# The values of four attention heads projected at once, with 512 columns, in a one-core decoder layer

## The chip, the cores and the metric

The kernel runs on one core of a Trainium2 chip. The metric is the device time of one execution in microseconds (us). Before the change three executions took 487.59, 487.79 and 489.74 us (median 487.79). In the text PE is the matrix engine, DVE the vector engine, ACT the scalar engine, POOL the GpSimd engine, SP the queue that issues nearly all DMA transfers.

## The reference, cut to what matters

One layer of a decoder on 512 rows of 1024 numbers, in float32. The normalized input is multiplied by one wide matrix `w_in`, whose columns are queries, keys, values and gates of two kinds of attention and two gates for the merge:

```python
h = rms_norm(x, norm_g[i])
proj = h @ w_in[i]
dq, dk, dv, dg, mq, mk, mv, mg, gates = split_in_proj(proj)   # 512 columns each, gates 2048
o_a = diff_attention(dq, dk, dv, lam, lam_init, subln_g[i]) * jax.nn.silu(dg)
y_a = o_a @ w_branch_diff[i]
o_b = moba_attention(mq, mk, mv) * jax.nn.silu(mg)
y_b = o_b @ w_branch_moba[i]
g_a, g_b = jnp.split(gates, N_BRANCHES, axis=-1)
merged = jax.nn.sigmoid(g_a) * y_a + jax.nn.sigmoid(g_b) * y_b
x = x + merged @ w_out[i]
x = x + jax.nn.sigmoid(x @ w_ple_gate[i]) * (p[i] @ w_ple[i])
return rms_norm(x, final_g)
```

The differential attention has 4 heads, each with two softmax maps over 64 dimensions and values of 128 columns (so 512 columns of values in all). The other kind (MoBA) has 8 heads of 64 dimensions; with 512 rows its selection reduces to causal attention, and the kernel treats two of its heads together.

## The kernel before, in words

**Three products for one.** Every float32 operand is split into a high part, rounded by a copy on ACT (`split`, `split_later`, line 102), and a low part, the rest, by a subtraction (line 104) on DVE or POOL. A product is then three matmuls (`mm3`, lines 115 to 117): high by high, high by low, low by high.

**Stages.** First the per-layer embedding product and the norm of `x`, four tiles of 128 rows; each normalized tile `h` is transposed on PE (line 362), and split into `hThi` and `hTlo`. Then eight pairs `j` = 0 to 7 (four differential heads, then four pairs of MoBA heads): for each, three tiles k, q and gate are projected (`project`, `proj_T`, 24 matmuls of 512 columns each), and k and q are rotated on DVE (`qk_tile`, lines 460 to 463, a rope of four instructions), split and copied between halves of the partitions on ACT and DVE (lines 468 to 483). After that come the merge gates, the branch products, the output product and the gated embedding.

**Values before.** `proj_v` makes the values of two differential heads or two pairs of MoBA heads with 256 columns: the transposed input is stationary, the weights move, 24 matmuls for each of four tiles of rows. The values of heads 0 and 1 are made whole ahead of pair 0, while the input tiles are still being normalized (`v_hook` transposes the next tile in the midst of it). Of the three others one half (two tiles of rows, 48 matmuls) stands ahead of each of the pairs 1 to 6. Ahead of pair 7 stands the first gate tile, `("a", 0)`.

**What sets the order.** The program is written out by a small clock: each group of matmuls of a projection calls `step()`, which ticks the clock and lets waiting generators go on: splits of weights, ropes, and `attention`. A tick is three matmuls of 512 columns, or six of 256. The attention of pair `j` starts two ticks after `project(j)`, and is laid between the projections of what follows, by `PLAN` (line 35): S0 to S3 are the score products of the four row tiles (lines 507, 509), E0 to E3 their maximum on DVE (line 517) and exponential on ACT (line 522), N0 to N3 the normalization on DVE (lines 527, 559, 560), T0 to T3 the transposes of the result on PE (line 533), and a number is a wait of so many ticks. After T3 and 5 ticks follow the product with the values (line 592), and the norm of the head (lines 596 to 609). Each engine executes its own instructions in the order in which they were written. So the number of ticks between two pairs decides where on DVE and ACT the work of one pair falls between that of the other: 32 for pairs 1 to 7 before the change (8 of values or gate tile and 24 of k, q and gate).

**Weights.** `units` lists the weight tiles of 512 KB in the order of use. `pump_loads` keeps up to six of them loaded by SP, `pump_split` splits them into five pairs of buffers, three tagged w and two tagged v; a unit is split when its tag has a free buffer. Up to the start of pair 0 the low part is made on DVE, then on POOL.

**PSUM.** Banks are shared by name: three `pj` for projections, two `sc` for scores, two `tp` for transposes, one `av`.

Of the kernel before, what the change touches and what calls it, by code (L numbers as in the profile page):

```python
# [12 lines left out]
AF = mybir.ActivationFunctionType  # L13
ALU = mybir.AluOpType

P = 128
S = 512
D = 1024
NT = S // P
# [22 lines left out]
def hybrid_block(ctx, tc, x, p, norm_g, w_in, lq1, lk1, lq2, lk2, subln_g, w_bd, w_bm,  # L42
# [15 lines left out]
    def bank(tag):  # L58
        return ps.tile([P, 512], F32, tag=tag, name=tag, bufs=BANKS[tag])
# [5 lines left out]
    def spawn(gen, after=0):  # L65
        running.append([clock[0] + after, gen])
# [47 lines left out]
    def mm3(acc, ahi, alo, bhi, blo, start, stop):  # L114
        T.matmul(acc, ahi, bhi, start=start, stop=False)  # L115
        T.matmul(acc, ahi, blo, start=False, stop=False)  # L116
        T.matmul(acc, alo, bhi, start=False, stop=stop)  # L117
# [4 lines left out]
    def add(key, tag, pieces, kn, cn):  # L122

        index[key] = len(units)
        units.append((tag, pieces, kn, cn))

    def add_cols(key, tag, c0):
        add(key, tag, [(0, KT, w_in[:, c0:c0 + P])], KT, P)

    def add_v(kind, jj):  # L130
        c0 = (C_DV, C_MV)[kind] + jj * 256
        for u in range(2):
            add(("v", kind, jj, u), "v", [(0, 4, w_in[u * 512:(u + 1) * 512, c0:c0 + 256])], 4, 256)

    def add_qkg(j, tags="www"):
        for n in (1, 0, 2):
            c0 = ((C_DQ, C_DK, C_DG), (C_MQ, C_MK, C_MG))[j // 4][n] + (j % 4) * P
            add(("qkg"[n], j), tags[n], [(0, KT, w_in[:, c0:c0 + P])], KT, P)
# [2 lines left out]
        while True:  # L141
            yield from "wwwvv"

    add_v(0, 0)
    add_qkg(0)
    for j in range(1, 7):
        if j % 2:
            add_v(*divmod((j + 1) // 2, 2))
        add_qkg(j)
    tags = tag_cycle()  # L150
    add_cols(("a", 0), next(tags), C_GA)
    add_qkg(7, [next(tags) for _ in range(3)])
    order = [(n, m) for m in range(3) for n in "ab"][1:] + [("o", m) for m in range(3)]
    order += [(n, m) for m in range(3, 8) for n in "abo"]
# [14 lines left out]
    def pump_loads(most=RAW):  # L169
        while state["loaded"] < min(len(units), state["split"] + RAW) and most:  # L170
            tag, pieces, kn, cn = units[state["loaded"]]
            r = wraw.tile([P, 1024], F32, name="raw").rearrange("p (k n) -> p k n", n=cn)
            for k0, k, src in pieces:
                Y.dma_start(r[:, k0:k0 + k], src.rearrange("(k p) n -> p k n", p=P))
            raw[state["loaded"]] = r
            state["loaded"] += 1
            most -= 1
# [35 lines left out]
    def step():  # L213

        since[0] += 1
        if since[0] >= PUMP and pump_split():
            since[0] = 0
        tick()

    def use(key):  # L220
        u = index[key]
        while ready.get(u) != 2:
            if state["split"] <= u:
                pump_split()
            tick()
        return parts[u]

    def free(key):
        free_bufs[units[index[key]][0]] += 1
# [8 lines left out]
    def proj_T(acc, key):  # L238
        w = use(key)
        for k in range(KT):  # L240
            mm3(acc, w[0][:, k], w[1][:, k], hThi[:, k], hTlo[:, k], k == 0, k == KT - 1)
            step()
        free(key)

    def proj_v(v, kind, jj, ts_, hook=None):

        heads = 4 if kind else 2
        keys = [("v", kind, jj, u) for u in range(2)]
        ws = [use(key) for key in keys]
        vt = v.rearrange("p (t h n e) -> p t h n e", t=NT, h=heads, n=2)  # L250
        for t in ts_:
            acc = bank("pj")[:, :256]
            ts = slice(t * P, (t + 1) * P)
            for k in range(KT):
                mm3(acc, hThi[:, k, ts], hTlo[:, k, ts], ws[k // 4][0][:, k % 4], ws[k // 4][1][:, k % 4],
                    k == 0, k == KT - 1)
                if k % 2:
                    step()
                if hook and k == KT // 2:
                    hook(t, False)  # L260
            spawn(split_later(vt[:, t, :, 0], vt[:, t, :, 1], acc.rearrange("p (h e) -> p h e", h=heads)))
            if hook:
                hook(t, True)
        if NT - 1 in ts_:
            for key in keys:
                free(key)

    def v_tile():
        return vbig.tile([P, 2048], F32R, name="v")

# [5 lines left out]
    with tc.tile_pool(name="norm", bufs=2) as npool:  # L276
# [17 lines left out]
        load_x(0)  # L294
        load_x(1)
        Y.dma_start(gb, norm_g[0:1].broadcast_to([P, D]))
        pump_loads(1)
        load_x(2)
        pump_loads(1)
        load_x(3)  # L300
        pump_loads()
        Y.dma_start(ropet, rope.rearrange("c p s -> p c s"))
# [133 lines left out]

        hook = {}
        since[0] = -4
        v = v_tile()
        proj_v(v, 0, 0, range(NT), v_hook)  # L440

        V.tensor_scalar(gsub, gsub, 0.5 * (1.0 - LAM_INIT), None, op0=ALU.mult)
        lsc = npool.tile([P, HD], F32, name="lsc", bufs=1)
# [103 lines left out]
    def attention(kind, j, qkg, v):  # L547

        q, k, g = qkg
        sm = [Softmax(q, k, i) for i in range(NT)]  # L550
        pts = [pt_tiles() for _ in range(1 + kind)]

        def norm(i):
            e, rc = sm[i].e, sm[i].recip()
            if kind:
                for s in range(2):
                    V.tensor_scalar(e[s], e[s], rc[:, s:s + 1], 0.5, op0=ALU.mult, op1=ALU.mult)
            else:
                V.tensor_scalar(e[1], e[1], rc[:, 1:2], nlam, op0=ALU.mult, op1=ALU.mult)
                V.scalar_tensor_tensor(e[0], e[0], rc[:, 0:1], e[1], op0=ALU.mult, op1=ALU.add)  # L560

        def trans(i):
            for s in range(1 + kind):
                acc = p_transposed(sm[i].e[s], i)
                spawn(split_later(pt_q(pts[s][0], i), pt_q(pts[s][1], i), acc), after=1)

        for op in PLAN.split():
            if op[0] == "S":
                sm[int(op[1])].scores()
            elif op[0] == "E":  # L570
                sm[int(op[1])].exps()
            elif op[0] == "N":
                norm(int(op[1]))
            elif op[0] == "T":
                trans(int(op[1]))
            else:
                yield int(op)
        last = NT - 1
        if kind:
            for s in range(2):  # L580
                acc = bank(("av", "tp")[s])
                vp = v.rearrange("p (t h e) -> p t h e", t=NT, h=4)[:, :, 2 * (j % 2) + s]
                for m, (kb, n) in enumerate([(kb, n) for n in range(2) for kb in range(last)] + [(last, 0), (last, 1)]):
                    T.matmul(acc[:, kb * P:], vp[:, kb], pt_k(pts[s][n], kb), start=m == 0, stop=m == 2 * NT - 1)
                spawn(moba_out(j, s, acc, g[0], sm[3].e[s]), after=1)
                yield AV_LAG
            return
        acc = bank("av")
        vp = v.rearrange("p (t h n e) -> p t h n e", t=NT, h=2, n=2)[:, :, j % 2]
        ab = ((0, 0), (1, 0), (0, 1))  # L590
        for m, (kb, a, b) in enumerate([(kb, *n) for n in ab for kb in range(last)] + [(last, *n) for n in ab]):
            T.matmul(acc[:, kb * P:], vp[:, kb, a], pt_k(pts[0][b], kb), start=m == 0, stop=m == 3 * NT - 1)  # L592
        yield SUB_LAG[0]

        sq = sm[3].e[0]
        A.activation(sq, acc, AF.Square)
        V.scalar_tensor_tensor(oraw[j], acc, gsub, g[0], op0=ALU.mult, op1=ALU.mult)
        yield SUB_LAG[1]
        tot = bank("tp")
        for i in range(NT):  # L600
            T.matmul(tot[:, 2 * i:2 * i + 2], sq[:, i * P:(i + 1) * P], ones, start=True, stop=True)
        yield SUB_LAG[2]
        rstd = pow_half(tot[:, 0:2 * NT:2], P, SUBLN_EPS, NT)
        yield SUB_LAG[3]
        rb = bank("tp")
        for i in range(NT):
            T.transpose(rb[:, i * P:(i + 1) * P], rstd[:, i:i + 1].to_broadcast([P, P]), ident)
        yield SUB_LAG[4]
        V.tensor_mul(oraw[j], oraw[j], rb)
# [8 lines left out]
    def project(j):  # L618
        qkg = [[], [], []]
        for n in (1, 0, 2):  # L620
            acc = bank("pj")
            proj_T(acc, ("qkg"[n], j))
            spawn(gate_tile(acc, qkg[n]) if n == 2 else qk_tile(acc, "qk"[n], qkg[n]))
        return qkg


    vs = [v]
    lo_engine[0] = G
    for j in range(7):
        if j:  # L630
            h = (j + 1) // 2
            if j % 2:
                vs.append(v_tile())
            proj_v(vs[h], h // 2, h % 2, (0, 1) if j % 2 else (2, 3))
        spawn(attention(j // 4, j % 4, project(j), vs[j // 2]), after=2)
    acc = bank("pj")
    proj_T(acc, ("a", 0))
    A.activation(oraw[7], acc, AF.Copy)
    spawn(attention(1, 3, project(7), vs[3]), after=2)

# [239 lines left out]
```

## Time and profile before

| | us |
|---|---|
| three executions | 487.59, 487.79, 489.74 |
| profiled execution, whole | 489.9 |
| its span, first to last instruction | 487.8 |
| PE busy | 478.5 (98% of the span) |
| DVE busy | 293.5 (60%) |
| ACT busy | 244.2 (50%) |
| POOL busy | 118.8 (24%) |

The page of the profile gives shares by engine, the span in 40 slices, and the chain of work that ended last. Starts are counted from the first instruction. The ends of matmuls are modelled, since they are pipelined: the rate of PE is read from the distance between two starts, not from the length of one. A releaser in brackets names what ended the idle time before an instruction.

### The profile page before, as it was taken

What the parts mean: (1) busy time and instruction counts of PE and PEld (TensorE: products, weight loads), DVE (VectorE), ACT (ScalarE), POOL (GpSimd) and SP (SyncE); (2) the same over time, 40 slices, a digit from 0 to 9 for tenths busy, and PEclk for the clock granted to TensorE, in tenths of its full rate; (3) what the DMA queues carried; (4) which work ended last, traced back from release to release, by engine and by line L of the source; (5) the groups of instructions that cost most, each with busy time, mean ns of one, the idle gap of its engine ahead of it and who ended that gap; (6) DMA issues with size and microseconds to landing.
All of it is one profiled execution on the core that took longest, in us unless ns stands there. A gap on an engine that the chain in (4) does not pass through costs nothing.

```text
span 487.8 us, 6678 instructions
## 1 busy us (share of the span) xinstructions
PE 478.5 (98%) x2485; PEld 409.8 (84%) x2485; DVE 293.5 (60%) x625; ACT 244.2 (50%) x521; POOL 118.8 (24%) x104
## 2 busy tenths in 40 slices
PE   8999999999999999999999999999999999999994
PEld 7898989889898898988888888888888888888884
DVE  3776686877868669677786447543344345343565
ACT  4665755575646657556677445422422232222442
POOL 1105543542344424425547430000000000000001
PEclk9999999999999999999999999999999999999998
DMA  8964341232114311211234313423322393200013
GB/s 266 338 182 131 92 125 44 86 98 77 45 45 128 88 44 45 86 44 44 88 91 122 90 45 90 126 86 103 113 87 87 97 324 96 86 1 0 2 43 129
DMA packets 63535, 47.73 MB, mean 98 GB/s; under 512 B 2320, under 2 KB 56848, under 8 KB 63504
## 3 DMA queue, kind: packets, MB, share of 16 engines
q1 hardware_dynamic: 63360, 47.06, 31.4%
q8 instruction: 19, 0.31, 0.3%
q10 hardware_dynamic: 144, 0.26, 0.1%
q14 instruction: 12, 0.10, 0.1%
HBM read 45.22 MB, written 2.10 MB: 97 GB/s over the span
## 4 chain that ended last, share of the span: by engine, by line
PE 97%; issue 1%; DVE 1%; ACT 0%; POOL 0%; POOLq 0%; DVEq 0%; ACTq 0%
PE pj L115 18%; PE pj L117 18%; PE pj L116 18%; PE sc L115 4%; PE sc L117 4%; PE sc L116 4%; PE tp L115 3%; PE tp L117 3%; PE tp L116 3%; PE tp L533 3%; PE sc L509 2%; PE sc L507 2%; PE av L117 2%; PE av L115 2%; PE av L116 2%; PE av L592 2%
## 5 line engine op out<-in xcount | busy, mean ns | idle before, releaser
L104 POOL TENSOR_TENSOR wl<-raw,wh 128x512 fp32r<-128x512 f32 x54 | 71.8, 1346 | 96.4 <-ACT wh L102 96.1
L115 PE MATMUL pj<-hThi,wh 128*128 128x512 f32 x232 | 93.0, 401 | 0.0
L117 PE MATMUL pj<-hThi,wl 128*128 128x512 f32 x232 | 90.9, 392 | 0.0
L116 PE MATMUL pj<-hTlo,wh 128*128 128x512 f32 x232 | 90.6, 390 | 0.0
L102 ACT ACTIVATE wh<-raw 128x512 fp32r<-128x512 f32 x96 | 56.8, 625 | 20.0 <-PE tp L117 17.0
L111 POOL TENSOR_TENSOR ry<-rv,mhalf 128x1 f32<-128x1 f32 (+1 forms) x11 | 8.6, 778 | 231.2 <-DVE rv L110 231.2
L522 ACT ACTIVATE sc<-sc,nm 128x128 f32<-128x128 f32 (+3 forms) x64 | 35.5, 556 | 33.2 <-DVE nm L517 33.2
L117 PEld LDWEIGHTS pj<-hThi,wl 128*128 128x128 f32 x232 | 43.6, 188 | 9.5
L116 PEld LDWEIGHTS pj<-hTlo,wh 128*128 128x128 f32 x232 | 43.7, 188 | 8.0
L104 DVE TENSOR_TENSOR wl<-raw,wh 128x512 fp32r<-128x512 f32 x42 | 27.8, 687 | 37.6 <-ACT wh L102 37.5
L115 PEld LDWEIGHTS pj<-hThi,wh 128*128 128x128 f32 x232 | 43.7, 188 | 7.8
L115 PE MATMUL pj<-vh,hThi 128*128 128x256 f32 (+1 forms) x136 | 40.0, 294 | 0.1
L517 DVE CUSTOM_DVE_ANT_0 sc<-sc,mask 128x128 f32<-128x128 f32 (+3 forms) x64 | 28.7, 486 | 18.5 <-PE sc L509 18.4
L117 PE MATMUL pj<-vh,hTlo 128*128 128x256 f32 (+1 forms) x136 | 39.1, 288 | 0.0
L116 PE MATMUL pj<-vl,hThi 128*128 128x256 f32 (+1 forms) x136 | 39.1, 288 | 0.0
L104 DVE TENSOR_TENSOR ptl<-tp,pth 128x128 fp32r<-128x128 f32 (+3 forms) x48 | 22.0, 486 | 23.9 <-ACT pth L102 23.8
L104 DVE TENSOR_TENSOR vl<-raw,vh 128x512 fp32r<-128x512 f32 x28 | 18.6, 686 | 28.2 <-ACT vh L102 28.2
L102 ACT ACTIVATE vh<-raw 128x512 fp32r<-128x512 f32 x48 | 28.2, 624 | 12.9 <-issue 8.6
L104 POOL TENSOR_TENSOR vl<-raw,vh 128x512 fp32r<-128x512 f32 x20 | 25.9, 1308 | 24.8 <-ACT vh L102 24.8
L102 ACT ACTIVATE pth<-tp 128x128 fp32r<-128x128 f32 (+3 forms) x48 | 19.0, 430 | 16.9 <-PE tp L533 16.7
L115 PEld LDWEIGHTS pj<-vh,hThi 128*128 128x128 f32 x136 | 25.8, 190 | 0.8 <-issue 0.3
L116 PEld LDWEIGHTS pj<-vl,hThi 128*128 128x128 f32 x136 | 25.9, 190 | 0.6
(283 smaller groups left out, 1057.5 us busy)
## 6 DMA issues: line engine op xcount, KB each, us to landing
raw<-in_w_in_dram SPq DMA_DIRECT2D x48, 512.0 KB, 3.8
raw<-in_w_out_dram SPq DMA_DIRECT2D x8, 512.0 KB, 3.9
raw<-in_w_ple_gate_dram SPq DMA_DIRECT2D x8, 512.0 KB, 3.8
xt<-in_x_dram SPq DMA_DIRECT2D x4, 512.0 KB, 8.4
raw<-in_w_branch_diff_dram SPq DMA_DIRECT2D x8, 256.0 KB, 2.8
raw<-in_w_branch_moba_dram SPq DMA_DIRECT2D x8, 256.0 KB, 3.3
xs<-in_x_dram SPq DMA_DIRECT2D x1, 2048.0 KB, 10.5
out_dram<-o SPq DMA_DIRECT2D x3, 512.0 KB, 2.6
```

The source lines that it names most:

```text
L102: A.activation(hi, src, AF.Copy)
L104: (eng or V).tensor_sub(lo, src, hi.bitcast(F32))
L111: G.tensor_tensor(out=y, in0=v, in1=mhalf[:, :cols], op=ALU.pow)
L115: T.matmul(acc, ahi, bhi, start=start, stop=False)
L116: T.matmul(acc, ahi, blo, start=False, stop=False)
L117: T.matmul(acc, alo, bhi, start=False, stop=stop)
L507: T.matmul(self.accs[s][:, :kv], qs_[:, s, qs], ks_[:, s, :kv], start=True, stop=False)
L509: T.matmul(self.accs[s][:, :kv], qs_[:, s, qs], kl[:, s, :kv], start=False, stop=True)
L517: V.tensor_tensor_reduce(out=self.e[s], in0=self.accs[s][:, :kv], in1=mask[:, 384 - i * P:384 - i * P + kv], op0=ALU.add, op1=ALU.min, sca ...
L522: A.activation(self.e[s], self.e[s], AF.Exp, bias=self.nm[:, s:s + 1], scale=-1.0, accum_out=self.sm[:, s:s + 1])
L533: T.transpose(acc[:, kb * P:(kb + 1) * P], e[:, kb * P:(kb + 1) * P], ident)
L592: T.matmul(acc[:, kb * P:], vp[:, kb, a], pt_k(pts[0][b], kb), start=m == 0, stop=m == 3 * NT - 1)
```

## The change

All 512 columns of differential values are projected by a new function, `proj_v_all`, ahead of pair 0: 24 matmuls of 512 columns for each of the four tiles of rows, and two value tiles are filled. Their weights come as four units of 256 rows by 512 columns, and a unit is freed in the last tile of rows as soon as it has been read. The MoBA values keep their 256 columns and their halves, which now stand ahead of pairs 4 to 7 instead of 3 to 6. The gate tile `("a", 0)` stands ahead of pair 2 instead of pair 7. The ticks between pairs become 24, 32, 24, 32, 32, 32, 32 for pairs 1 to 7. Two weight loads instead of one are issued ahead of the third input tile, and two more ahead of the fourth.

```diff
--- before.py
+++ after.py
@@ -127,6 +127,10 @@
     def add_cols(key, tag, c0):
         add(key, tag, [(0, KT, w_in[:, c0:c0 + P])], KT, P)
 
+    def add_v_all():
+        for u, tag in enumerate("vvww"):
+            add(("va", u), tag, [(0, 2, w_in[u * 256:(u + 1) * 256, C_DV:C_DV + 512])], 2, 512)
+
     def add_v(kind, jj):
         c0 = (C_DV, C_MV)[kind] + jj * 256
         for u in range(2):
@@ -141,14 +145,18 @@
         while True:
             yield from "wwwvv"
 
-    add_v(0, 0)
-    add_qkg(0)
-    for j in range(1, 7):
-        if j % 2:
-            add_v(*divmod((j + 1) // 2, 2))
-        add_qkg(j)
+    add_v_all()
+    add_qkg(0, "wvv")
+    add_qkg(1)
+    add_cols(("a", 0), "v", C_GA)
+    add_qkg(2)
+    add_qkg(3)
+    add_v(1, 0)
+    add_qkg(4)
+    add_qkg(5)
+    add_v(1, 1)
+    add_qkg(6)
     tags = tag_cycle()
-    add_cols(("a", 0), next(tags), C_GA)
     add_qkg(7, [next(tags) for _ in range(3)])
     order = [(n, m) for m in range(3) for n in "ab"][1:] + [("o", m) for m in range(3)]
     order += [(n, m) for m in range(3, 8) for n in "abo"]
@@ -265,6 +273,28 @@
             for key in keys:
                 free(key)
 
+    def proj_v_all(vs, hook):
+
+        ws = [use(("va", u)) for u in range(2)]
+        for t in range(NT):
+            acc = bank("pj")
+            ts = slice(t * P, (t + 1) * P)
+            for k in range(KT):
+                if k // 2 == len(ws):
+                    ws.append(use(("va", k // 2)))
+                mm3(acc, hThi[:, k, ts], hTlo[:, k, ts], ws[k // 2][0][:, k % 2], ws[k // 2][1][:, k % 2],
+                    k == 0, k == KT - 1)
+                step()
+                if k == KT // 2:
+                    hook(t, False)
+                if t == NT - 1 and k % 2:
+                    free(("va", k // 2))
+            for n, v in enumerate(vs):
+                vt = v.rearrange("p (t h n e) -> p t h n e", t=NT, h=2, n=2)
+                spawn(split_later(vt[:, t, :, 0], vt[:, t, :, 1],
+                                  acc[:, n * 256:(n + 1) * 256].rearrange("p (h e) -> p h e", h=2)))
+            hook(t, True)
+
     def v_tile():
         return vbig.tile([P, 2048], F32R, name="v")
 
@@ -294,9 +324,9 @@
         load_x(0)
         load_x(1)
         Y.dma_start(gb, norm_g[0:1].broadcast_to([P, D]))
-        pump_loads(1)
+        pump_loads(2)
         load_x(2)
-        pump_loads(1)
+        pump_loads(2)
         load_x(3)
         pump_loads()
         Y.dma_start(ropet, rope.rearrange("c p s -> p c s"))
@@ -436,8 +466,8 @@
 
         hook = {}
         since[0] = -4
-        v = v_tile()
-        proj_v(v, 0, 0, range(NT), v_hook)
+        vs = [v_tile(), v_tile()]
+        proj_v_all(vs, v_hook)
 
         V.tensor_scalar(gsub, gsub, 0.5 * (1.0 - LAM_INIT), None, op0=ALU.mult)
         lsc = npool.tile([P, HD], F32, name="lsc", bufs=1)
@@ -624,19 +654,17 @@
         return qkg
 
 
-    vs = [v]
     lo_engine[0] = G
-    for j in range(7):
-        if j:
-            h = (j + 1) // 2
-            if j % 2:
+    for j in range(8):
+        if j == 2:
+            acc = bank("pj")
+            proj_T(acc, ("a", 0))
+            A.activation(oraw[7], acc, AF.Copy)
+        elif j >= 4:
+            if j % 2 == 0:
                 vs.append(v_tile())
-            proj_v(vs[h], h // 2, h % 2, (0, 1) if j % 2 else (2, 3))
+            proj_v(vs[-1], 1, j // 2 - 2, (0, 1) if j % 2 == 0 else (2, 3))
         spawn(attention(j // 4, j % 4, project(j), vs[j // 2]), after=2)
-    acc = bank("pj")
-    proj_T(acc, ("a", 0))
-    A.activation(oraw[7], acc, AF.Copy)
-    spawn(attention(1, 3, project(7), vs[3]), after=2)
 
 
 
```

Three places show how instructions move. Line numbers of the changed kernel are 30 higher from `proj_v_all` on.

On ACT, ahead of the values: before, the split of the second input tile (`hThi` from `tp_272`) follows the square of the third.

```order
L102 ACTIVATE vh_289<-raw_122 128x512 x2
L348 ACTIVATE sq_297,ss_298<-xt_106 128x1024
L337 ACTIVATE ple_91<-pj_173 128x512
L369 ACTIVATE hThi_89<-tp_272 128x4x128
L369 ACTIVATE hThi_89<-tp_277 128x4x128
```

In the changed kernel the same place reads:

```order
L102 ACTIVATE vh_289<-raw_121 128x512 x2
L378 ACTIVATE sq_297,ss_298<-xt_106 128x1024
L367 ACTIVATE ple_91<-pj_173 128x512
L102 ACTIVATE wh_322<-raw_124 128x512 x2
L102 ACTIVATE wh_336<-raw_126 128x512 x2
L399 ACTIVATE hThi_89<-tp_272 128x4x128
L399 ACTIVATE hThi_89<-tp_277 128x4x128
```

Four split copies of the two further units (`wh_322`, `wh_336`) stand ahead of that tile's split now.

On DVE, between E3 and N3 of pair 0 (in both listings `tp_804` is the result of T1, `rc` the start of a normalization), before; `pj_738` is the k tile of pair 1.

```order
L559 TENSOR_SCALAR sc1_2_747<-sc1_2_747,rc_800,lam_97 128x384
L560 SCALAR_TENSOR_TENSOR sc0_2_746<-sc0_2_746,rc_800,sc1_2_747 128x384
L104 TENSOR_TENSOR ptl_652<-tp_804,pth_651 128x2x128
L460 STREAM_SHUFFLE qr_818<-pj_738 128x512
L461 TENSOR_TENSOR pj_738<-pj_738,ropet_95 128x512
L462 TENSOR_TENSOR qr_818<-qr_818,ropet_95 128x512
L463 TENSOR_TENSOR pj_738<-pj_738,qr_818 128x512
L527 RECIPROCAL rc_830<-sm_789 128x2
L559 TENSOR_SCALAR sc1_3_791<-sc1_3_791,rc_830,lam_97 128x512
L560 SCALAR_TENSOR_TENSOR sc0_3_790<-sc0_3_790,rc_830,sc1_3_791 128x512
```

In the changed kernel (`pj_650` is the k tile, `pj_730` the q tile of pair 1):

```order
L589 TENSOR_SCALAR sc1_2_737<-sc1_2_737,rc_800,lam_97 128x384
L590 SCALAR_TENSOR_TENSOR sc0_2_736<-sc0_2_736,rc_800,sc1_2_737 128x384
L509 TENSOR_TENSOR kl_807<-pj_650,ks_780 64x512 x2
L104 TENSOR_TENSOR ptl_665<-tp_804,pth_664 128x2x128
L490 STREAM_SHUFFLE qr_825<-pj_730 128x512
L491 TENSOR_TENSOR pj_730<-pj_730,ropet_95 128x512
L492 TENSOR_TENSOR qr_825<-qr_825,ropet_95 128x512
L493 TENSOR_TENSOR pj_730<-pj_730,qr_825 128x512
L557 RECIPROCAL rc_839<-sm_788 128x2
L589 TENSOR_SCALAR sc1_3_790<-sc1_3_790,rc_839,lam_97 128x512
L590 SCALAR_TENSOR_TENSOR sc0_3_789<-sc0_3_789,rc_839,sc1_3_790 128x512
```

The rope of the q tile has come ahead of N3, and the low part of k ahead of `ptl` of T1; the rope of the k tile, which stood here, has moved up, ahead of E3.

```order
L490 STREAM_SHUFFLE qr_755<-pj_650 128x512
L491 TENSOR_TENSOR pj_650<-pj_650,ropet_95 128x512
L492 TENSOR_TENSOR qr_755<-qr_755,ropet_95 128x512
L493 TENSOR_TENSOR pj_650<-pj_650,qr_755 128x512
L104 TENSOR_TENSOR ptl_665<-tp_746,pth_664 128x128
L547 ISA sc0_3_789,nm_787<-sc_748,mask_81 128x512
L547 ISA nm_787 128x1
L547 ISA sc1_3_790,nm_787<-sc_749,mask_81 128x512
```

On ACT at the same place, before (`pth` from `tp_804` is the high part of T1's result):

```order
L522 ACTIVATE sc0_3_790,sm_789<-sc0_3_790,nm_788 128x512
L522 ACTIVATE sc1_3_791,sm_789<-sc1_3_791,nm_788 128x512
L102 ACTIVATE pth_651<-tp_804 128x2x128
L102 ACTIVATE wh_815<-raw_524 128x512 x2
L468 ACTIVATE ks_848<-pj_738 64x512 x2
```

In the changed kernel:

```order
L498 ACTIVATE ks_780<-pj_650 64x512 x2
L102 ACTIVATE wh_778<-raw_535 128x512
L552 ACTIVATE sc0_3_789,sm_788<-sc0_3_789,nm_787 128x512
L552 ACTIVATE sc1_3_790,sm_788<-sc1_3_790,nm_787 128x512
L502 ACTIVATE ks_780<-ks_780 64x512 x2
L513 ACTIVATE kl_807<-kl_807 64x512 x2
L102 ACTIVATE pth_664<-tp_804 128x2x128
```

The copies of k (lines 498, 502 and 513, before the change 468, 472 and 483) have come ahead of the copy of T1's result.

## Rows read from the trace of the kernel before

**Rows 1.** The page, chain that ended last: shares of the span.

```profile
PE 97%; issue 1%; DVE 1%; ACT 0%; POOL 0%; POOLq 0%; DVEq 0%; ACTq 0%
```

**Rows 2.** Timeline of PE: start us, us, engine line op out<-in shapes xcount.

```profile
31.93 0.28 PE L115 MATMUL pj<-vh,hThi 128*128 128x256 f32 x1
...
35.40 0.28 PE L117 MATMUL pj<-vh,hTlo 128*128 128x256 f32 x1
35.52 0.40 PE L115 MATMUL pj<-hThi,wh 128*128 128x512 f32 x1
...
51.64 0.39 PE L117 MATMUL pj<-hThi,wl 128*128 128x512 f32 x1
```

**Rows 3.** Timeline of PE, the first projection of values.

```profile
21.37 0.36 PE L115 MATMUL pj<-vh,hThi 128*128 128x256 f32 x1
...
30.70 1.04 PE L362 MATMUL tp<-ident,h 128*128 128x128 f32 x8
31.49 0.36 PE L115 MATMUL pj<-vh,hThi 128*128 128x256 f32 x1
```

**Rows 4.** The input tiles xt: their loads, and from issue to landing.

```profile
L284 SPq DMA_DIRECT2D xt<-in_x_dram x4: 432/543/1857, 3.7 to 7.9; - x4
...
DMA to landing us min/median/max: 6.3/8.4/10.9
```

**Rows 5.** Timeline of PE, attention of pair 0: S2 and T3.

```profile
57.10 0.51 PE L507 MATMUL sc<-ks,qs 128*128 128x384 f32 x2
...
71.84 0.60 PE L533 MATMUL tp<-ident,sc 128*128 128x128 f32 x4
```

**Rows 6.** Timeline of DVE, the same stretch.

```profile
57.95 0.55 DVE L517 CUSTOM_DVE_ANT_0 sc<-sc,mask 128x384 f32<-128x384 f32 x1
...
59.66 0.48 DVE L560 SCALAR_TENSOR_TENSOR sc<-sc,rc,sc 128x256 f32<-128x256 f32 x1
...
61.04 0.68 DVE L517 CUSTOM_DVE_ANT_0 sc<-sc,mask 128x512 f32<-128x512 f32 x1
...
63.52 0.62 DVE L560 SCALAR_TENSOR_TENSOR sc<-sc,rc,sc 128x384 f32<-128x384 f32 x1
...
69.20 0.15 DVE L527 RECIPROCAL rc<-sm 128x2 f32<-128x2 f32 x1
...
70.03 0.75 DVE L560 SCALAR_TENSOR_TENSOR sc<-sc,rc,sc 128x512 f32<-128x512 f32 x1
...
71.56 1.40 DVE L479 TENSOR_TENSOR kl<-pj,ks 64x512 fp32r<-64x512 f32 x2
...
73.00 0.74 DVE L460 STREAM_SHUFFLE qr<-pj 128x512 f32<-128x512 f32 x1
...
75.10 0.70 DVE L463 TENSOR_TENSOR pj<-pj,qr 128x512 f32<-128x512 f32 x1
```

**Rows 7.** Timeline of ACT, the same stretch.

```profile
60.02 0.62 ACT L102 ACTIVATE wh<-raw 128x512 fp32r<-128x512 f32 x1
...
61.76 0.72 ACT L522 ACTIVATE sc<-sc,nm 128x512 f32<-128x512 f32 x1 [0.44 <-DVE nm L517]
...
65.50 0.39 ACT L102 ACTIVATE pth<-tp 128x256 fp32r<-128x256 f32 x1 [2.21 <-PE tp L533]
...
69.32 1.22 ACT L468 ACTIVATE ks<-pj 64x512 fp32r<-64x512 f32 x2 [2.17 <-DVE pj L463]
...
71.08 1.29 ACT L472 ACTIVATE ks<-ks 64x512 fp32r<-64x512 f32 x2
72.39 1.28 ACT L483 ACTIVATE kl<-kl 64x512 fp32r<-64x512 f32 x2
```

**Rows 8.** Timeline of DVE, one operation in pairs 0 and 1.

```profile
56.63 0.36 DVE L559 TENSOR_SCALAR sc<-sc,rc,lam 128x128 f32<-128x128 f32 x1
...
85.36 1.42 DVE L559 TENSOR_SCALAR sc<-sc,rc,lam 128x128 f32<-128x128 f32 x1
```

**Rows 9.** Timeline of POOL, beside the second of these.

```profile
84.16 2.53 POOL L104 TENSOR_TENSOR wl<-raw,wh 128x512 fp32r<-128x512 f32 x2
```

## The prediction

> **What bounds the kernel now.** I read the page first, and there the chain of work that ended last: PE is 97% of it [rows 1]. So the time is the number of matmuls times the distance between their starts, plus the places where PE waits. Next I read PE's timeline for those distances. The first and the last row of the k, q and gate tiles of pair 0 are 72 matmuls of 512 columns without a gap, 71 steps from 35.52 to 51.64: 0.227 us each. Thirty of 256 columns, 29 steps from 31.93 to 35.40, take 0.1197 us each [rows 2]. Two matmuls of 256 columns thus cost 0.2394 us and one of 512 columns 0.2270: the wider one saves 0.0124 us. Third, I looked for the places where PE waits. After the start only the first projection of values has them: from 21.37 to the first matmul of k at 35.52 are 14.15 us, of which 96 matmuls at 0.1197 are 11.49 and two groups of transposes at 0.79 (30.70 to 31.49) are 1.58 [rows 2, 3]. The rest, 1.08 us, is waiting for the splits of the input and of the weights. From there to the merge gates PE is the chain's only engine. So I then followed, on DVE and ACT, what has to end before T3 of pair 0, since the change takes ticks from there.
>
> **The values at once.** Removed are 192 matmuls of 256 columns (two times 96), added 96 of 512. At 0.0124 us for each of the 96 that is 1.2 us less [rows 2]. This is PE's own time on the chain, so it counts in full.
>
> [...]
>
> **The waits of the first projection.** Four units are split ahead of it instead of two: four more half-unit copies on ACT, 0.62 us each [rows 7], 2.5 us, and as many subtractions on DVE, all ahead of the second input tile's split. But PE's first tile of rows takes 24 x (0.227 - 0.1197) = 2.6 us longer [rows 2], so the second tile is late by nothing that PE feels. In the three later tiles PE has about twice the time, while transposing, splitting and scaling the next tile take no longer than before. I expect 0.2 us of the 1.08 to stay, a gain of 0.9. Bounds: 1.08 gained, or 1.0 lost if the four further copies, or a late load, hold up the second tile. The loads speak little against it: the four input tiles land from 3.7 + 6.3 = 10.0 to 7.9 + 10.9 = 18.8 us, and with six pieces of 512 KB from the first landing to the last, one piece is 1.5 us [rows 4]. The third tile goes behind one more piece, the fourth behind two, so the last lands at about 21.8. Its square on ACT stands behind the second tile's split, later than that. The k tile of pair 0 now uses buffers of the first value unit; they are freed after 6 of the last 24 matmuls, so 18 x 0.227 = 4.1 us remain for a split of two halves (0.62 on ACT and about as much on DVE for each). I cost that at nothing; without that cover it would be about 2 us once.
>
> **Pairs 1 and 3 lose their 8 ticks.** The work of PE is the same, only moved, and so far worth nothing. But attention of pairs 0 and 2 is now filled by 24 ticks, and in the order of DVE and ACT the k and q tiles of the next pair come 8 ticks sooner, between S2 and T3. I count from S2's first matmul in pair 0.
>
> PE: before, T3 starts 71.84 - 57.10 = 14.74 us after S2 [rows 5]. Six matmuls of 512 columns now stand where 12 of 256 stood, 0.07 less: PE would be ready at 14.67.
>
> DVE: E2 and N1 end at 59.66 + 0.48 = 60.14, that is 3.04 after S2 [rows 5, 6]. Now the rope of k comes next, 73.00 to 75.80, 2.80 us [rows 6]; it ends at 5.84.
>
> ACT then, in its new order: copies of k 1.22, half a weight 0.62, the two exponentials of E3 1.44, the copies to the other half 1.29 and those of the low part 1.28, and only then the copy of T1's result, 0.39 [rows 7]. Sum 6.24, so 12.08. (E3's maxima and the low part of k are done on DVE meanwhile.)
>
> DVE waits for that copy at its `ptl` of T1, and queued behind it stand the rope of q and N3: `ptl` about as long as the copy, 0.39, the rope 2.80, N3 from 69.20 to 70.78, 1.58 [rows 6, 7]. N3 ends at 16.85, and T3 needs it. PE waits 16.85 - 14.67 = 2.2 us.
>
> Bounds. If ACT's detour cost nothing, DVE alone would need 3.10 for E3 and N2 (61.04 to 64.14), 1.40 for the low part of k, then 0.39 + 2.80 + 1.58 as above [rows 6, 7]: 5.84 + 9.27 = 15.11, a wait of 0.4. Upward, DVE beside POOL is the unknown: the same operation took 0.36 us in pair 0 and 1.42 in pair 1, where it ended at 86.78, with POOL's two subtractions from 84.16 to 86.69 [rows 8, 9]. In the changed order POOL has weights to split there too. The rope's product of two SBUF tiles and N3's scaling could each lose such 1.06 us: 4.3. I take 2.2, what the rows sum to.
>
> The same in the window of pair 2. There DVE has the last multiplication of pair 1's head too (128x512, about the 0.70 of a rope's addition [rows 6]), partly under S2: I add 0.5, 2.7. Bounds 0.4 and 4.8.
>
> After T3, PE has six matmuls (1.36 us) to the next pair's S0. It needs the low part of q, which on DVE stands behind `ptl` of T2: 1.40 for the low part and some 0.5 ahead of it. I take 0.2 of waiting each time, 0.4. In the windows of pairs 1 and 3, with 32 ticks, DVE catches up; I cost them at nothing. Pairs 4 to 7 keep 32 ticks, and the gate tile that moved is 24 matmuls here or there.
>
> **The sum.** -1.2 - 0.9 + 2.2 + 2.7 + 0.4 = +3.2 us. The profiled execution took 489.9 (487.8 and 2.1 around its span), so 493.1 for it; that one execution is 2.1 above the median shown. On the median: 487.8 + 3.2 = 491.0 us, 0.7% more. From no change a measurement can tell 0.5%, 2.4 us.
>
> **Rivals.**
>
> The other side: DVE and ACT keep up. Before, the engines have time to spare in this stretch: ACT waited 2.21 us for PE at T1's result and 2.17 for DVE at the copy of k [rows 7], so an earlier start can eat slack. If the waits at T3 are the lower bound, 0.4 each, the time is 487.8 - 2.1 + 0.8 = 486.5; if none comes, 485.7, not slower. It decides at 1.0 us of waiting for each window: below that the gain of the values wins. Against it stands that all of DVE's work from S2 on is now one queue with no gap, which the new order shows, and that even without ACT the sum lies 0.4 above PE. Chance 0.27.
>
> POOL blocks DVE. With one such 1.06 us in each window, 491.0 + 2.1 = 493.1; with both in each, 495.2. For it: rows 8 and 9. Against it: N3 took 1.58 in pair 0, with its scaling at no more than 0.68 of that, so mostly POOL is not in the way. Chance 0.13.
>
> [...]
>
> More than the sum of gains: no waits at T3 at all, all 1.08 us at the front, and a few groups of matmuls that follow each other with less of a step where they change. That needs 485.3 or less. Chance 0.08.
>
> **The numbers.** The forecast has 0.52; its own range is 489.3 (waits of 1.5 and 1.5) to 492.6. Of that about 0.40 lies above 490.2, more than 0.5% slower; with the POOL rival 0.53. Within 0.5% are the other 0.12 and the first rival's 0.27, 0.39. Faster has 0.08. The range goes from 485.7, where no wait comes, to 493.5, a little beyond the POOL rival's first case; 0.1 or so is left out on each side.
>
> **What would show it.** Right: matmuls of 512 columns in the first projection at 0.227 us and its end (first matmul of k) at 21.37 + 96 x 0.227 + 1.58 + 0.2 = 44.9; at T3 of pairs 0 and 2 a gap on PE of some 2 us that ended with DVE's line 590 (N3); on DVE at `ptl` of T1 a wait for ACT's copy. Pairs 4 to 7 as long as before. Wrong: PE without a gap at T3, or a gap at another place, as at S0 of a pair (low part of q), at the first weights of pair 0 (buffers of the value units), or in the MoBA pairs, which I cost at nothing.

## The result, and the profile after

The changed kernel took 494.01 us (median of 6 runs, 493.48 to 496.36), the kernel before beside it 488.59 (487.59 to 489.74): the ratio is 1.0133, 95% interval 1.0115 to 1.0152. The direction was as forecast, the size about double, and the time lies above the range.

Executions of both kernels fall into two groups some 2 us apart (before 487.59 to 487.79 and 489.38 to 489.74, after 493.48 to 494.03 and 495.46 to 496.36), and the two traces differ by 2.7 us ahead of the first matmul of the values (21.37 in before, 18.63 in after), so beside the ratios the text compares stretches of a trace from that matmul on. From there to the end before's trace has 487.75 - 21.37 = 466.4 us [rows 3], that of after 491.48 - 18.63 = 472.85: 6.5 us more.

The page of after, the granted clock in 40 slices and the chain that ended last [rows 1]:

```profile
PEclk9999999999989999999999999999999999999998
...
PE 88%; DVE 5%; ACT 3%; issue 2%; DMA 1%; POOL 0%; POOLq 0%; SPq 0%; DVEq 0%; ACTq 0%
```

PE is no longer alone on the chain, and one slice in the midst has a clock below 9. The timeline of PE (start us, us, engine, line, operation, in brackets the idle time before and what ended it) at the first projection's start, the first matmul of k, T3 of pair 0, S0 of pair 1, and T3 of pair 2:

```profile
18.63 0.48 PE L115 MATMUL pj<-vh,hThi 128*128 128x512 f32 x1
...
42.52 0.39 PE L115 MATMUL pj<-hThi,vh 128*128 128x512 f32 x1
...
80.65 0.63 PE L563 MATMUL tp<-ident,sc 128*128 128x128 f32 x4 [1.94 <-DVE sc L590]
...
82.94 0.30 PE L537 MATMUL sc<-ks,qs 128*128 128x128 f32 x1 [0.22 <-ACT wh L102]
...
137.87 1.09 PE L563 MATMUL tp<-ident,sc 128*128 128x128 f32 x4 [3.67 <-DVE sc L590]
```

The first stage takes 23.89 us to the first matmul of k. Before it was 14.15 [rows 2, 3], and 96 matmuls of 0.1197 that stood later, 11.49: 25.64. So 1.75 are won. Then PE waits 1.94 and 3.67 for line 590 (line 560 in the kernel before), where before it had no wait at T3 [rows 5]. Counted from start to start, less the usual step of 0.227, these are 2.10 and 3.83. At S0 of pair 1 the wait counted so is 0.34; the bracket names ACT, but S0 does not read `wh`. The low part of q on DVE (81.39, two operations in 1.41) ends at 82.80, 0.14 ahead of PE's row, as N3's end at 80.50 is 0.15 ahead of T3.

What DVE and ACT do ahead of T3 of pair 0. ACT first, then DVE:

```profile
71.88 0.71 ACT L552 ACTIVATE sc<-sc,nm 128x512 f32<-128x512 f32 x1
...
72.71 1.29 ACT L502 ACTIVATE ks<-ks 64x512 fp32r<-64x512 f32 x2
74.02 1.28 ACT L513 ACTIVATE kl<-kl 64x512 fp32r<-64x512 f32 x2
75.33 0.38 ACT L102 ACTIVATE pth<-tp 128x256 fp32r<-128x256 f32 x1
```

```profile
72.98 1.40 DVE L509 TENSOR_TENSOR kl<-pj,ks 64x512 fp32r<-64x512 f32 x2
75.75 0.43 DVE L104 TENSOR_TENSOR ptl<-tp,pth 128x256 fp32r<-128x256 f32 x1 [1.36 <-ACT pth L102]
...
79.75 0.75 DVE L590 SCALAR_TENSOR_TENSOR sc<-sc,rc,sc 128x512 f32<-128x512 f32 x1
```

The exponentials, 2.57 us of copies of k, then the copy of T1's result; DVE stands 1.36 us for it, with the rope of q and N3 behind. Now the same stretch of pair 2, DVE and POOL. On DVE the first two rows are N0, the third is the end of pair 1's head, then two rows of the rope of k, the end of N2, and `ptl` of T1:

```profile
118.02 1.46 DVE L589 TENSOR_SCALAR sc<-sc,rc,lam 128x128 f32<-128x128 f32 x1
119.52 1.28 DVE L590 SCALAR_TENSOR_TENSOR sc<-sc,rc,sc 128x128 f32<-128x128 f32 x1
120.72 0.67 DVE L639 TENSOR_TENSOR o<-o,tp 128x512 f32<-128x512 f32 x1
...
123.95 0.70 DVE L491 TENSOR_TENSOR pj<-pj,ropet 128x512 f32<-128x512 f32 x1
124.55 1.26 DVE L492 TENSOR_TENSOR qr<-qr,ropet 128x512 f32<-128x512 f32 x1
...
128.58 1.73 DVE L590 SCALAR_TENSOR_TENSOR sc<-sc,rc,sc 128x384 f32<-128x384 f32 x1
...
133.00 0.42 DVE L104 TENSOR_TENSOR ptl<-tp,pth 128x256 fp32r<-128x256 f32 x1 [1.36 <-ACT pth L102]
```

```profile
116.85 2.54 POOL L104 TENSOR_TENSOR wl<-raw,wh 128x512 fp32r<-128x512 f32 x2
119.36 1.29 POOL L104 TENSOR_TENSOR vl<-raw,vh 128x512 fp32r<-128x512 f32 x1
123.97 1.29 POOL L104 TENSOR_TENSOR vl<-raw,vh 128x512 fp32r<-128x512 f32 x1 [3.32 <-ACT vh L102]
128.60 1.30 POOL L104 TENSOR_TENSOR vl<-raw,vh 128x512 fp32r<-128x512 f32 x1 [3.34 <-ACT vh L102]
```

Each long DVE row ends shortly after a POOL row: 119.48 after 119.39, 120.80 after 120.65, 125.81 after 125.26, 130.31 after 129.90. The last of them costs nothing: pair 0 has its like (1.75 at 71.32), and in both pairs DVE still waits 1.36 for ACT after it. What sets pair 2 apart is the beginning: counted from S2's first matmul (63.88 and 118.89) the rope of k starts at 2.75 in pair 0 and at 4.42 in pair 2, 1.67 later, and its long product adds 0.58.

What follows the long wait stands in the windows of after: the stretch, its length, busy time of PE, PEld, DVE, ACT and POOL, granted clock, DMA share, GB/s.

```profile
133.00:137.26 4.26, 1.20 (x6) 0.66 (x4) 4.15 (x9) 2.09 (x4) 2.95 (x2) 1.00 0.23 66
137.26:140.67 3.41, 2.80 (x13) 2.83 (x14) 3.00 (x5) 2.86 (x6) 1.29 (x1) 0.50 0.25 74
140.67:145.00 4.33, 4.33 (x35) 4.24 (x35) 2.64 (x13) 2.46 (x10) 2.59 (x2) 1.00 0.39 121
```

For 3.41 us (137.26 to 140.67) the granted clock was 0.50; PE's first row in it is T3. From T3's row to 140.67, where the clock rose, are 2.80 us; the same matmuls take 1.54 in a run below that kept the full clock (135.50 to 137.04, without POOL): 1.26 more.

### The profile page after: what moved, and what is told of

It reads as the page before. It is cut to its first block, busy times and chain, and to the rows that moved or that the text cites. A ratio compares the mean times of both kernels' runs of the same rounds, so it can differ in the third digit from the quotient of the medians.

```text
span 491.5 us, 6489 instructions
## 1 busy us (share of the span) xinstructions
PE 476.5 (97%) x2389; PEld 403.4 (82%) x2389; DVE 294.9 (60%) x627; ACT 244.1 (50%) x521; POOL 116.7 (24%) x102
## 4 chain that ended last, share of the span: by engine, by line
PE 88%; DVE 5%; ACT 3%; issue 2%; DMA 1%; POOL 0%; POOLq 0%; SPq 0%; DVEq 0%; ACTq 0%
PE pj L115 16%; PE pj L117 16%; PE pj L116 16%; PE sc L115 4%; PE sc L117 4%; PE sc L116 4%; PE tp L117 3%; PE tp L115 3%; PE tp L116 3%; PE tp L563 2%; PE av L117 2%; PE av L115 2%; PE av L116 2%; PE sc L537 2%; PE sc L539 2%
## 5 line engine op out<-in xcount | busy, mean ns | idle before, releaser
L115 PE MATMUL pj<-hThi,wh 128*128 128x512 f32 x208 | 84.0, 404 | 0.0
L117 PE MATMUL pj<-hThi,wl 128*128 128x512 f32 x208 | 81.5, 392 | 0.0
L116 PE MATMUL pj<-hTlo,wh 128*128 128x512 f32 x208 | 81.3, 391 | 0.0
L117 PEld LDWEIGHTS pj<-hThi,wl 128*128 128x128 f32 x208 | 39.1, 188 | 8.6
L116 PEld LDWEIGHTS pj<-hTlo,wh 128*128 128x128 f32 x208 | 39.2, 189 | 6.8
L115 PE MATMUL pj<-vh,hThi 128*128 128x256 f32 (+1 forms) x96 | 31.0, 323 | 0.0
L116 PE MATMUL pj<-vl,hThi 128*128 128x256 f32 (+1 forms) x96 | 30.6, 319 | 0.0
L117 PE MATMUL pj<-vh,hTlo 128*128 128x256 f32 (+1 forms) x96 | 30.5, 317 | 0.0
L563 PE MATMUL tp<-ident,sc 128*128 128x128 f32 x120 | 18.8, 277 | 5.6 <-DVE sc L590 5.6
L563 PEld LDWEIGHTS tp<-ident,sc 128*128 128x128 f32 x120 | 15.1, 143 | 10.0 <-issue 6.4
```

The costliest lines, as they stand in the source:

```text
L563: T.transpose(acc[:, kb * P:(kb + 1) * P], e[:, kb * P:(kb + 1) * P], ident)
```

## The experiments

Nine kernels ran, each beside runs of the kernel before. "Stretch" is the time from the first matmul of values to the end, less that of before (466.4); the waits are the bracketed ones of PE's rows. Of each edit against the changed kernel only the lines that matter are printed; `late` and `short` are true while pairs 1 and 3 are projected, `short` for the k tile alone.

| kernel | median us | ratio (95%) | stretch | T3 pair 0 | T3 pair 2 |
|---|---|---|---|---|---|
| changed | 494.01 | 1.0133 (1.0115 to 1.0152) | +6.5 | 1.94 | 3.67 |
| 256 columns at the front | 496.62 | 1.0172 (1.0149 to 1.0195) | +8.3 | 1.80 | 3.67 |
| late copies | 499.10 | 1.0226 (1.0201 to 1.0251) | +11.2 | none | 0.69 |
| filled wait | 493.00 | 1.0109 (1.0093 to 1.0126) | +5.5 | 1.93 | 0.51, behind the transposes |
| no POOL | 490.05 | 1.0044 (1.0031 to 1.0058) | +2.7 | 1.62 | 1.59 |
| second copies late | 491.11 | 1.0047 (1.0025 to 1.0070) | +2.3 | 0.77 | 2.50 |
| spread | 502.70 | 1.0295 (1.0254 to 1.0337) | +14.4 | none | none |
| both | 486.16 | 0.9969 (0.9952 to 0.9987) | -1.2 | none | none |
| gates early | 487.78 | 0.9972 (0.9955 to 0.9990) | -0.7 | none | none |
| fewer splits | 491.86 | 1.0053 (1.0037 to 1.0069) | +3.5 | 0.33 | 0.31 |

**256 columns at the front.**

```diff
-        proj_v_all(vs, v_hook)
+        proj_v(vs[0], 0, 0, range(NT), v_hook)
+        proj_v(vs[1], 0, 1, range(NT))
```

> As the changed kernel, but the values of the four differential heads are formed ahead of pair 0 by two projections with 256 columns (192 matmuls) instead of one with 512 (96). If the width saves what the rows of before say (0.0124 us for each of the 96 pairs), 1.2 us more than the changed kernel: 495.2 us; k of pair 0 starts some 1.2 us later after the first matmul of values than the 23.9 us there. Rival: the first projection is bound by the splits of the input tiles and not by the matmuls, then the same 494.0.

```profile
21.05 0.36 PE L115 MATMUL pj<-vh,hThi 128*128 128x256 f32 x1
...
46.72 0.40 PE L115 MATMUL pj<-hThi,vh 128*128 128x512 f32 x1
```

25.67 us where 512 columns took 23.89: 1.8 more. 192 matmuls at 0.1197 are 22.98 and 96 at 0.227 are 21.79, so the width gives its 1.2; the other 0.6 are waits (25.67 - 22.98 - 1.58 = 1.11, in the changed kernel 0.52). Both waits at T3 are still there, and the stretch is longer by the same 1.8: what was lost has nothing to do with the width.

**Late copies.** All of k's copies on ACT, and its low part on DVE, 4 ticks later in pairs 1 and 3.

```diff
-        yield QK_LAG[0]
+        yield QK_LAG[0] + (4 if tag == "k" and late[0] else 0)
```

> As the changed kernel, but in pairs 1 and 3 ACT's copies of k (and the low part of k) come 4 ticks later, behind the copy of T1's result. Theory (ACT's detour through the copies of k keeps DVE waiting at ptl of T1): the wait at T3 falls from 2.1 to 0.4 or less in pair 0, and from 3.8 to under 1.5 in pair 2, where the granted clock then does not fall: 487.5 to 489. [...]

PE at T3 of pair 0 and S0 of pair 1, then the chain ahead of that S0 on ACT and on DVE:

```profile
81.19 0.60 PE L563 MATMUL tp<-ident,sc 128*128 128x128 f32 x4
...
85.94 0.45 PE L537 MATMUL sc<-ks,qs 128*128 128x128 f32 x1 [2.06 <-DVE qs L509]
```

```profile
81.42 1.35 ACT L513 ACTIVATE kl<-kl 64x512 fp32r<-64x512 f32 x2 [2.70 <-DVE kl L509]
```

```profile
84.54 0.56 DVE L104 TENSOR_TENSOR ptl<-tp,pth 128x384 fp32r<-128x384 f32 x1 [2.43 <-ACT pth L102]
```

A miss: 499.10, 10 us over the theory's 489. T3 of pair 0 is free, as the detour through ACT wants, but the low part of k now comes behind N3, ACT's last copy waits 2.70 us for it, DVE then 2.43 for ACT, and PE 2.06 at S0. The clock fell too, to 0.50 from 85.82 to 92.64. Pair 3 goes the same way, with 2.02 at its S0. A second fall there is an estimate: the run's mean clock is 0.986, which at 0.50 makes 14.0 of its 498.9 us, and the first fall is 6.82 of them and the end of the run 2.4, as in before. So the edit put back the chain that it should have eased; it shows that ACT's copies hold T3 up, and not what a good order gains.

**Filled wait.** 28 transposes of the identity ahead of T3 of pair 2.

```diff
+        for n in range(extra):
+            T.transpose(acc[:, (n % 4) * P:(n % 4 + 1) * P], ident, ident)
```

> As the changed kernel, but PE does 28 transposes of the identity, some 2.8 us, in the wait ahead of T3 of pair 2; they go into the bank that T3 writes afterwards, and nobody reads them. Theory (the granted clock fell to half because PE had stood still for 3.8 us, and that cost 1.2 to 1.3 us more): T3 starts at the same time, the clock stays full, and the time is 492.7. Rival: the fall has another cause, or costs nothing on the path: 494.0; if the transposes reach past the wait, more.

```profile
134.53 3.22 PE L564 MATMUL tp<-ident 128*128 128x128 f32 x28
138.26 0.66 PE L566 MATMUL tp<-ident,sc 128*128 128x128 f32 x4 [0.51 <-DVE sc L593]
```

T3 starts as late as before, but the clock stays at 1.00 (133.00 to 145.00). From T3 to the sums of the head's norm (line 631, 634 here) after has 151.31 - 137.87 = 13.44 us, this kernel 150.87 - 138.26 = 12.61. Of the 1.26 that the slow stretch took, 0.8 comes back; 0.36 is a wait at S0 of pair 3, which the slow matmuls had covered. With the wait filled no fall came, where the changed kernel had 0.50 for 3.41 us: there it followed from the wait.

**No POOL.** No low parts of the weights that are split while pairs 1 and 3 are projected: `low` is false there, and the high part stands in for the low one.

```diff
-            yield from split_later(hi[:, ks], lo[:, ks], src, LO_LAG, lo_engine[0])
+            if low:
+                yield from split_later(hi[:, ks], lo[:, ks], src, LO_LAG, lo_engine[0])
+            else:
+                A.activation(hi[:, ks], src, AF.Copy)
+                yield LO_LAG
```

> As the changed kernel, but of the weight tiles that are split while pairs 1 and 3 are projected the low part is left out (the high part is used in its place), so POOL has nothing to do in the windows of pairs 0 and 2. Theory (POOL's subtractions lengthen DVE's work in pair 2's window): the wait at T3 of pair 2 falls from 3.8 to about 2, as in pair 0, where it stays 1.8 to 2.1, and the clock does not fall: about 490.5 to 491. Rival (ACT's detour alone): both waits stay, 494.0.

PE at T3 of pairs 0 and 2, then the two operations of DVE that took 1.46 and 1.28 in the changed kernel:

```profile
80.79 0.63 PE L571 MATMUL tp<-ident,sc 128*128 128x128 f32 x4 [1.62 <-DVE sc L598]
...
135.50 0.63 PE L571 MATMUL tp<-ident,sc 128*128 128x128 f32 x4 [1.59 <-DVE sc L598]
```

```profile
118.20 0.35 DVE L597 TENSOR_SCALAR sc<-sc,rc,lam 128x128 f32<-128x128 f32 x1
118.58 0.35 DVE L598 SCALAR_TENSOR_TENSOR sc<-sc,rc,sc 128x128 f32<-128x128 f32 x1
```

Both take 0.35, and the two windows become alike. POOL was 2.1 us of pair 2's wait, 0.3 of pair 0's, and the 0.49 at S3 of pair 2 (below) and the fall of the clock went with it: 3.8 us of the stretch in all. This is the expected size.

**Second copies late.** In pairs 1 and 3 the copies of k to the other half, and of its low part, behind the copy of T1's result; the low part as early as before.

```diff
-        if tag == "k":
+        if tag == "k" and not short:
...
-            yield QK_LAG[1]
+            yield 3 if short else QK_LAG[1]
+            if short:
+                for s, (own, other) in enumerate(HEADS):
+                    A.activation(st[other, s], st[own, s].bitcast(F32), AF.Copy)
```

> As the changed kernel, but in pairs 1 and 3 only the copies of k to the other half of the partitions (and those of its low part) come later, behind ACT's copy of T1's result; the low part itself is formed as early as before. Theory (DVE waits at ptl of T1 because ACT makes 2.6 us of these copies first): no wait at T3 of pair 0 (2.1 in the changed kernel), under 1.5 at T3 of pair 2 (3.8), no fall of the clock, some 0.7 at S0 instead of 0.34: about 489.0. Rival (the chain through k and q to S0 of the next pair is as long, so that a wait only changes its place, as with all copies late): over 2 us at S0, 492.5 or more.

```profile
79.97 0.63 PE L567 MATMUL tp<-ident,sc 128*128 128x128 f32 x4 [0.77 <-DVE sc L594]
...
135.58 0.63 PE L567 MATMUL tp<-ident,sc 128*128 128x128 f32 x4 [2.50 <-DVE sc L594]
```

Each wait is 1.2 shorter, no wait turns up at S0, and behind T3 of pair 2 the matmuls of 256 columns have their usual step of 0.12 (136.16 to 136.28), where it was 0.21 in the changed kernel. In all that is 4.2 us of the stretch. More stays at both places than I expected.

**Both.** The two edits above together.

> The last two edits together on the changed kernel: no low parts of the weights that are split while pairs 1 and 3 are projected (left out, so POOL has nothing to do there), and the second copies of k behind T1's copy. If POOL and ACT's detour are all there is: no wait over 0.5 at T3 of pairs 0 and 2, some 0.7 at S0, 490.05 - 1.78 - 1.75 + 0.7 = 487.2. Rival: DVE's own work in 24 ticks is too long without either, 1 us or more at each T3, 489 or more.

```profile
81.14 0.60 PE L575 MATMUL tp<-ident,sc 128*128 128x128 f32 x4
...
133.89 0.60 PE L575 MATMUL tp<-ident,sc 128*128 128x128 f32 x4
```

Neither T3 waits, and the time is below that of before: 0.9969. It leaves low parts out, so it is no kernel to use; but ACT's detour and POOL are the whole of the waits at T3; DVE's own work fits into 24 ticks.

**Fewer splits.** The second copies late, and a weight half every 5 ticks instead of 3.

```diff
-        if since[0] >= PUMP and pump_split():
+        if since[0] >= PUMP + 2 * late[0] and pump_split():
```

> The second copies of k behind T1's copy, as in that run, and the halves of weight tiles are split every 5 ticks instead of every 3 while pairs 1 and 3 are projected, so POOL subtracts less often beside DVE; nothing is left out. [...] Rival (the splits only come later and hold PE up at the weights, or meet DVE elsewhere): no gain, 491 or more.

```profile
135.05 0.63 PE L568 MATMUL tp<-ident,sc 128*128 128x128 f32 x4 [0.31 <-DVE sc L595]
136.62 0.30 PE L542 MATMUL sc<-ks,qs 128*128 128x128 f32 x1 [0.94 <-DVE qs L511]
137.34 0.30 PE L542 MATMUL sc<-ks,qs 128*128 128x128 f32 x1 [0.43 <-ACT vh L102]
```

The waits at T3 all but go, and waits at S0 of pair 3 take their place, and others of 0.53 and 0.24 for POOL in the norm of two heads. The median is 491.86, beside 491.11 with the second copies late alone, where I forecast 489.5 from fewer subtractions beside DVE. No gain, as the rival said.

**Spread.** No window of 24 ticks, but four of 28.

```diff
-        if j == 2:
+        if j in (1, 2):
             acc = bank("pj")
-            proj_T(acc, ("a", 0))
+            proj_T(acc, ("a", 0), 4 * j - 4, 4 * j)
...
-            proj_v(vs[-1], 1, j // 2 - 2, (0, 1) if j % 2 == 0 else (2, 3))
+            proj_v(vs[-1], 1, int(j > 4), [(0, 1), (2, 3), (0, 1), (2,), (3,)][j - 3])
```

> The values at once, as in the changed kernel, but no window of 24 ticks: the first gate tile is formed in two halves of 4 ticks ahead of pairs 1 and 2 (added up later), the MoBA values come with 8, 8, 8, 4 and 4 ticks ahead of pairs 3 to 7. Theory (only the short windows cost): pair 0's wait of 2.1 goes with 4 ticks of 0.68 us, no waits, the gain at the front (1.75 us) stays: 487.6 - 1.75 = 485.9, up to 486.4. Rival (a window of 28 ticks is short too, about 1 us in each of the four): 489.9.

The product with the values of pair 0, and T3 of MoBA pairs 5 and 6:

```profile
84.93 0.68 PE L623 MATMUL av<-pth,v 128*128 128x512 f32 x2 [1.70 <-ACT pth L102]
...
227.80 1.12 PE L564 MATMUL tp<-ident,sc 128*128 128x128 f32 x4 [3.35 <-DVE ptl L104]
...
260.27 0.90 PE L564 MATMUL tp<-ident,sc 128*128 128x128 f32 x6 [3.29 <-DVE ptl L104]
```

A clear miss, the worst kernel of all. Four ticks fewer cost a differential pair 1.5 to 1.7 us at its product with the values, and a MoBA pair 3.3. Behind the wait of 3.35 the four transposes of T3 took 1.12; in the changed kernel four took 1.09 at a clock of 0.50 and 0.63 at 1.00. The run's mean clock is 0.991, that of before 0.997. At these two places T3 waits for a PSUM bank: its reader, `ptl` of T2, stands on DVE behind the rope of q, which four ticks less put ahead of it (the rope's last row starts at 226.59, `ptl` at 227.20, T3 at 227.80).

**Gates early.** Three gate tiles ahead of pairs 1 to 3, so that all windows have 32 ticks.

```diff
-        if j == 2:
+        if 1 <= j <= 3:
             acc = bank("pj")
-            proj_T(acc, ("a", 0))
-            A.activation(oraw[7], acc, AF.Copy)
+            proj_T(acc, (("a", 0), ("a", 1), ("b", 1))[j - 1])
+            A.activation((oraw[7], *early)[j - 1], acc, AF.Copy)
```

> The values at once, as in the changed kernel, and 32 ticks in every window: three gate tiles come ahead of pairs 1, 2 and 3 instead of one ahead of pair 2, two of them kept in a further 4 KB of each partition, for which one of the six load buffers is given up; behind pair 7 the later gate tiles move up by two. Theory (all that was lost came from the two short windows, the front kept its gain of 1.75 us): no wait at T3 of pairs 0 and 2, 487.6 - 1.75 = 485.9, faster than both. Rival (five load buffers or the changed order at the merge cost as much, or the gain at the front is lost later): 487.6 or more.

```profile
80.98 0.60 PE L565 MATMUL tp<-ident,sc 128*128 128x128 f32 x4
...
139.93 0.60 PE L565 MATMUL tp<-ident,sc 128*128 128x128 f32 x4
```

This version beats both kernels, though by less than the 1.75 us expected: 0.9972 of before (0.9955 to 0.9990), 1.4 us by the ratio and 0.7 by the stretch. The front keeps its gain (44.95 - 21.08 = 23.87 us to the first matmul of k); about 1 us of it is lost again at S3 of pairs 1 and 2, which start 0.5 late each; what holds them up was not followed.

## Why the prediction was half right

**The values at once: right.** The matmuls of 512 columns start 0.227 us apart, and with 256 columns the 1.2 us come back.

**The waits of the first projection: nearly.** 23.89 less 96 x 0.227 and the 1.58 of transposes [rows 3] leaves 0.52, where I expected 0.2 of 1.08.

**Pair 0: right, in place, size and cause.** 2.10 against 2.2, ended by N3, with DVE held at `ptl` of T1 by ACT's copy. The second copies late take 1.2 of it, POOL out of the way 0.3, both all of it.

**Pair 2: the step that failed.** "The same in the window of pair 2 ... I add 0.5, 2.7". It has 3.83 at T3, 0.49 more at S3 ahead of it and 1.26 of slow matmuls behind it, 5.6 in all. The wait at T3 alone lies inside my bounds of 0.4 and 4.8, the three together lie beyond them. The added 0.5 was for the end of pair 1's head, which without POOL costs nothing (1.59 in pair 2, 1.62 in pair 0); what lengthens the window is POOL. In either pair the long row at the end of N2 (1.75 and 1.73) is hidden by the wait for ACT, and only the rope's 0.96 instead of 0.68 shows in pair 0; in pair 2 the first two lengthened operations stand ahead of E2, and all that follows moves back. I had the mechanism as a rival, and turned it down with N3 of pair 0 alone [rows 6], beside which POOL ran only to 69.70, while the row that spoke for it [rows 8, 9] was the one that came true.

**The clock: not in the sum at all.** The upper end of my range counted waits only. The wait of 3.67, with the clock at 0.50 behind it, had a price of 1.26 us more, and no row of before showed one.

**S0 behind T3: right.** 0.34 in pair 1; in pair 3 it was covered by the slow matmuls, and 0.36 once these were gone.

**Pairs 4 to 7: right.** From the first matmul of the norm of pair 3's head to the end are 319.3 us (172.21 to 491.48), before 319.1 (168.66 to 487.75). The spread kernel shows what that rested on: with 28 ticks these pairs would have been the worst.

The sum with what was measured: -1.75 + 2.10 + 0.34 + 0.49 + 3.83 + 1.26 = 6.3 of the 6.5; the other 0.2 stands behind the norm of pair 3's head, and I did not trace it.

## What to carry to other kernels

Where a change moves work out of a window that hides another engine's chain, the wait is set by that chain's order on each engine, and in pair 0 it could be summed from rows (2.2 against 2.10); but a row in which one operation takes three or four times its usual time must be priced for every window, not only where it was seen: the same operation took 0.36 and 1.42 in two windows of before [rows 8], and 1.46 in pair 2's of after. A wait of PE can cost more than its length: the one of 3.67 us brought 1.26 of slow matmuls behind it, one of 2.50 none. And a filler that is taken from a window can be replaced by another: with gate tiles in the windows no wait came at T3, and 0.7 us of the front's 1.77 were left at the end; half the filler in four windows was worse than none in two.

## What was not expected of the hardware

**The clock after a wait.** In PE's wait of 3.67 us, at 137.26 and 0.61 ahead of T3, the granted clock fell to 0.50, for 3.41 us. Behind the wait of 1.94 it stayed at 1.00 (80.00 to 133.00), and behind one of 2.50 the matmuls had their usual step of 0.12 (second copies late). In the kernel with late copies one of 2.06, which came 3.7 us after another of 0.47, brought 0.50 from 85.82 to 92.64, and one of 2.02, behind two of 0.69, another fall by the estimate above; in the spread kernel the transposes behind the wait of 3.35 took 1.12 instead of 0.63. The length of a wait alone does not tell a fall here, as 2.50 and 2.06 show; what does was not shown. With 28 transposes that nobody reads in the wait of the changed kernel, the clock stayed at 1.00 (133.00 to 145.00).

**Which operations took longer beside POOL.** At 123.95 a product with one operand in PSUM took its usual 0.70 beside POOL (123.97 to 125.26), and the next, with both in SBUF, 1.26 instead of 0.68. That makes no rule: in before the 0.36 of [rows 8] fell beside POOL too (55.61 to 56.91). What decides it was not shown.

**The start.** In the profile of before the product of the embedding has 0.63 us for a matmul of 512 columns at 7.28, and the next starts 0.42 later; in that of after 0.39 at 6.24, and 0.23. The first matmul of values comes 2.7 us later in before (21.37 and 18.63). The trace's first record of a full clock is at 10.86 us in before and at 4.14 in after; ahead of it there is no record. The change is hardly the cause: in the kernel of **Both**, whose front is that of the changed one, PE comes to T3 of pair 0 at 81.14 without a wait there, in the changed one at 78.55 (80.65 less its 2.10). Why is open.

```profile
7.28 0.63 PE L331 MATMUL av<-pwh,pTh 128*128 128x512 f32 x1
```

```profile
6.24 0.39 PE L361 MATMUL av<-pwh,pTh 128*128 128x512 f32 x1
```
